# A decoder layer whose residual stream is laid out by features instead of by tokens, on one Trainium2 core

## The chip, the core and the metric

The kernel runs on one core of one Trainium2 chip. Its engines are TensorE (PE in the profile; PEld is its loading of the stationary operand), VectorE (DVE), ScalarE (ACT), GpSimd (POOL) and SyncE (SP), which here only issues DMAs. The metric is the device time of one execution in microseconds, the median of three runs.

## The reference

One layer on 1024 tokens with 1024 features, all in float32:

```
x = x + 0.5 * swiglu(rms_norm(x, ffn1_norm), w_gate, w_up, w_down)       # 2816 hidden
h = rms_norm(x, mix_norm)
q, k, v, f, sq, sk, sv, g_fox, g_sb = split(h @ w_in)
merged = sigmoid(g_fox) * (forgetting_attention(q, k, v, f) @ w_branch_fox)
       + sigmoid(g_sb) * (stick_breaking_attention(sq, sk, sv) @ w_branch_sb)
x = x + merged @ w_out
x = x + 0.5 * swiglu(rms_norm(x, ffn2_norm), ...)
x = x + sigmoid(rms_norm(x, ple_norm) @ w_ple_gate) * (p @ w_ple_proj)
rms_norm(x, g) = x * rsqrt(mean(x*x over features) + 1e-6) * g
```

There are four norms over features; each is followed by a product that sums over features. `p` has 256 columns.

## The kernel before

**Operands.** A product needs both operands with the summed dimension on the 128 partitions. To keep float32 accuracy each operand is split into a high part, rounded to the format that TensorE takes (`f32r`), and a low part, the difference; a product is high x high + high x low + low x high, three matmuls. ACT makes high parts by a copy (line 112, in line 136 for whole weight tiles), DVE or POOL the low parts by a subtraction (line 113, line 146).

**Layout.** The residual `X` is two tiles, one for each half of the tokens, with tokens on partitions: `[128 tokens, 4 token tiles, 1024 features]`. The normed activation is wanted with features on partitions. So for each tile of 128 tokens `norm_stat` squares the row on ACT (line 206, the sum comes with it), POOL adds EPS and raises to -0.5 (210, 211), `norm_mul` scales by the token's factor and the gain row on DVE (214), and `turn` transposes the eight 128x128 blocks on TensorE (219) into PSUM, from where `norm_post` (or `norm_high` and `norm_low`) splits them. The gain is loaded as a row spread over 128 partitions.

**Feed-forward.** Gate and up products and the down product use a Strassen-like scheme: seven products of blocks (numbers 1 to 7) for eight, with sums and differences of blocks of activations (`combo_a`, `_t`, `_l`, `_u`, `_s`, `_d`, `_e`) and of weights (`sums`, `last_sum`). `prep(n, m)` splits the weight operand of product `m` of weight block `n`; `product` issues its twelve matmuls (464), `plain` the first blocks without the scheme (419), which need the normed first half alone (`half` 0) and both halves' sums (`half` 1). Half 0 of the norm is called `N[0]`, half 1 `N[1]`; products on `N[1]` come later, so its norm stands between the first products.

**Down pass.** `make_down` runs seven steps for each of three chunks of hidden rows; a step has four `matmuls(t)` of twelve (359) and four `evict(t)` that add the bank to `X` (367, or 365 in the output projection, which uses the same code with one chunk). The stationary operand is the activation `act`, the moving one the weight `wt`, so the result has tokens on partitions. In the last chunk the norm of the next stage starts: statistics of half 0 at step 4, `norm_mul` at step 5, `norm_post` of half 0 and the statistics of half 1 at step 6. While the pass runs, the tail of the stage loads and splits the next weights (`load_v`, `split_v`, `ple_load`, `ple_split` and so on).

**Places of the norms.** Four stretches of the run are spoken of. A: the entry, `first_entry`, in which `p` is projected (`project`, 1208) while `x` is loaded and normed, and then `products`. B: the end of the first feed-forward, with the first units of `w_in` (`nat_steps`, 691) behind it. C: the output projection, `second_entry`, and `products`. D: the end of the second feed-forward, with the gate of the last stage behind it (`ple_steps`, 1490). In B and D the norm of half 1 is woven into the products of half 0 by `posts` and `weave`.

**Order.** From the entry of a feed-forward to the end of its tail the code runs under `manual_schedule`: each engine takes its instructions in the order in which they are written. Outside it (attention, the last eight gate units) a planner orders them, with TensorE's order pinned by `pe`. Tiles come from pools by tag; a tag has a fixed number of buffers (`BUFS`: PT 3, WL 3, H 4, Q, KH, KL, GF, RN 2), and a new tile waits for a free one.

## Time and profile before

| what | value |
|---|---|
| median of three runs | 2262.65 us (2262.49 to 2262.69) |
| profiled execution | 2262.69 us |
| its span in the trace | 2261.0 us |
| DMA | 276.01 MB, mean 122 GB/s |
| matmuls and transposes on TensorE | 11441 |

The profile comes from one execution. Its page gives the busy time of each engine, the chain of work that ended last, and groups of instructions by source line with their mean duration in ns and the idle time before them. In the view by time a row has start, duration, engine, line, operation and how many instructions were merged; in the chain in order of time a row has start, duration and what ran. Recorded matmuls overlap (389 ns each for 512 columns), so their spacing is what counts, not their duration. Busy time of PEld lies beside that of PE.

### The profile page before, as it was taken

The numbers are of one execution on the slowest core, as the hardware profiler recorded it, in microseconds if no ns is written. First come the engines' busy times: TensorE is split into PE (matmuls) and PEld (weight loads), VectorE is DVE, ScalarE is ACT, GpSimd is POOL, SyncE is SP. The second block draws the span as 40 slices with busy tenths as digits, with TensorE's granted clock in tenths as the row PEclk, the third lists the DMA queues.
The fourth block names the chain that finished last, engine by engine and source line by source line (L and its number), as shares of the span: only waits on it lengthen the run. The fifth ranks groups of instructions, "written<-read, shape, count | busy, mean of one in ns | idle before, by whom it ended". The sixth has DMA issues, their size and how long they took to land.

```text
span 2261.0 us, 30610 instructions
## 1 busy us (share of the span) xinstructions
PE 2243.2 (99%) x11441; PEld 1907.6 (84%) x11441; DVE 1468.5 (65%) x2206; ACT 975.4 (43%) x1740; POOL 820.2 (36%) x756
## 2 busy tenths in 40 slices
PE   9999999999999999999999999999999999999999
PEld 7888888888889999998988888888888888888887
DVE  7854545497873565656666676889655555778752
ACT  6433333343343555545456564246333333434431
POOL 1244444310024556645455654410544443200111
PEclk9999999999999999999999999999999999999999
DMA  7223232474432222222124236822423232756132
GB/s 261 79 94 117 90 120 84 163 282 147 164 125 56 77 85 71 75 62 75 43 71 117 62 121 206 304 104 61 140 84 126 84 126 80 261 194 216 62 101 93
DMA packets 186373, 276.01 MB, mean 122 GB/s; under 512 B 27112, under 2 KB 109288, under 8 KB 186224
## 3 DMA queue, kind: packets, MB, share of 16 engines
q1 hardware_dynamic: 186224, 274.05, 36.3%
q8 instruction: 90, 1.47, 0.3%
q14 instruction: 59, 0.48, 0.1%
HBM read 190.35 MB, written 75.27 MB: 117 GB/s over the span
## 4 chain that ended last, share of the span: by engine, by line
PE 95%; DVE 3%; ACT 1%; issue 1%; DMA 0%; POOL 0%; SPq 0%; POOLq 0%; DVEq 0%; ACTq 0%
PE ps L464 35%; PE ps L359 21%; PE ps L699 11%; PE ps L691 7%; PE ps L1490 4%; PE ps L1159 4%; PE ps L963 3%; PE ps L941 3%; PE ps L419 1%; PE ps L890 1%; PE ps L889 1%; PE ps L219 1%; PE ps L1208 1%; DVE RN L865 1%; DVE H L113 0%
## 5 line engine op out<-in xcount | busy, mean ns | idle before, releaser
L359 PE MATMUL ps<-H,H 128*128 128x512 f32 x2184 | 497.7, 389 | 1.2 <-DVE X L367 1.2
L359 PEld LDWEIGHTS ps<-H,H 128*128 128x128 f32 x2184 | 409.4, 188 | 86.7 <-issue 2.0
L464 PE MATMUL ps<-H,WL 128*128 128x512 f32 x1008 | 239.3, 389 | 0.8 <-ACT WL L112 0.8
L464 PEld LDWEIGHTS ps<-H,WL 128*128 128x128 f32 x1008 | 189.1, 188 | 40.5 <-ACT WL L112 1.2
L699 PE MATMUL ps<-H,WH 128*128 128x512 f32 x768 | 210.4, 401 | 1.0 <-DVE PT L814 1.0
L699 PEld LDWEIGHTS ps<-H,WH 128*128 128x128 f32 x768 | 136.2, 188 | 23.8 <-DVE PT L814 1.5
L146 POOL TENSOR_TENSOR WL<-Y,WH 128x512 fp32r<-128x512 f32 (+1 forms) x10 | 14.4, 1470 | 382.6 <-ACT WH L136 382.6
L944 DVE TENSOR_TENSOR PT<-ps,PT 128x512 fp32r<-128x512 f32 (+1 forms) x160 | 101.1, 633 | 73.0 <-ACT PT L943 71.8
L146 POOL TENSOR_TENSOR WL<-RAW,WH 128x512 fp32r<-128x512 f32 (+1 forms) x104 | 122.6, 1200 | 59.8 <-ACT WH L136 46.7
L464 PE MATMUL ps<-H,Q 128*128 128x512 f32 x600 | 143.1, 389 | 0.0
L367 DVE SCALAR_TENSOR_TENSOR X<-ps,X 128x512 f32<-128x512 f32 x168 | 109.1, 687 | 50.9 <-PE ps L359 50.9
L691 PE MATMUL ps<-WH,H 128*128 128x256 f32 (+1 forms) x896 | 132.9, 287 | 1.9 <-ACT RN L748 0.7
L464 PEld LDWEIGHTS ps<-H,Q 128*128 128x128 f32 x600 | 112.6, 188 | 23.4
L943 ACT CAST PT<-ps 128x512 fp32r<-128x512 f32 (+1 forms) x160 | 87.4, 549 | 93.6 <-PE ps L941 92.0
L464 PE MATMUL ps<-X,WL 128*128 128x512 f32 x504 | 121.1, 389 | 0.0
L691 PEld LDWEIGHTS ps<-WH,H 128*128 128x128 f32 x896 | 117.0, 190 | 4.0 <-PE ps L890 1.0
L464 PEld LDWEIGHTS ps<-X,WL 128*128 128x128 f32 x504 | 94.6, 188 | 19.6
L699 PE MATMUL ps<-H,WL 128*128 128x512 f32 x384 | 108.5, 399 | 0.0
L963 PE MATMUL ps<-PT,X 128*128 128x256 f32 (+1 forms) x640 | 104.1, 282 | 3.1 <-DVE PT L944 3.1
L963 PEld LDWEIGHTS ps<-PT,X 128*128 128x128 f32 x640 | 94.2, 190 | 14.6 <-DVE PT L944 5.3
L902 POOL TENSOR_TENSOR T<-T,l 128x128 f32<-128x128 f32 (+3 forms) x64 | 73.2, 1148 | 89.9 <-DVE l L901 87.5
L260 POOL TENSOR_TENSOR PT<-GF,RN 128x512 f32<-128x512 f32 x20 | 33.1, 1657 | 186.0 <-DVE GF L507 101.8
(402 smaller groups left out, 4719.7 us busy)
## 6 DMA issues: line engine op xcount, KB each, us to landing
hidden<-PT SPq DMA_DIRECT2D x40, 512.0 KB, 3.1
WH<-in_ffn_w_gate_dram SPq DMA_DIRECT2D x38, 512.0 KB, 4.8
Q<-hidden SPq DMA_DIRECT2D x24, 512.0 KB, 6.3
hidden<-RN SPq DMA_DIRECT2D x22, 512.0 KB, 2.6
RAW<-in_w_in_dram SPq DMA_DIRECT2D x22, 512.0 KB, 4.3
KH<-in_ffn_w_up_dram SPq DMA_DIRECT2D x20, 512.0 KB, 6.3
KL<-in_ffn_w_up_dram SPq DMA_DIRECT2D x20, 512.0 KB, 7.0
T<-in_ffn_w_down_dram SPq DMA_DIRECT2D x20, 512.0 KB, 4.6
```

What stands on the lines that cost most here:

```text
L146: ins = eng_lo.tensor_sub(lo[part], raw[part], f(hi[part]))
L359: pe(nc.tensor.matmul(groups[g][t][:], act[:, a, k, t * P:(t + 1) * P], wt[:, b, k, :], start=(fresh and n == 0), stop=(i in (6, 1, 4) and ...
L367: nc.vector.scalar_tensor_tensor(xs, groups[g][t][:], scale, xs, ALU.mult, ALU.add)
L464: pe(nc.tensor.matmul(ps[:], hl[:, a, k, :], rhs(m, b, k), start=(first and i == 0), stop=(final and i == 11), skip_group_check=True))
L691: pe(nc.tensor.matmul(ps[:, :n], hT[t // 4][a][:, k, (t % 4) * P:(t % 4 + 1) * P], w[k // 4][b][:, k % 4, :n], start=(i == 0), stop=(i == ...
L699: pe(nc.tensor.matmul(ps[:], w[a][:, k, :], hT[half][b][:, k, :], start=(i == 0), stop=(i == 23)))
L902: nc.gpsimd.tensor_mul(T[:, :n], T[:, :n], l[:].broadcast_to([P, n]))
L943: high = nc.scalar.copy(pt[:, 0, :width], ps[:, :width])
L944: low = nc.vector.tensor_sub(pt[:, 1, :width], ps[:, :width], f(pt[:, 0, :width]))
L963: pe(nc.tensor.matmul(o, lh, r, start=(kpair == c and i == 0), stop=(kpair == 0 and i == 3)))
L1159: pe(nc.tensor.matmul(ps[:], w[a][:, k, :], yT[g][b][:, k, half * 512:half * 512 + 512], start=(i == 0), stop=(i == 11)))
L1490: pe(nc.tensor.matmul(ps, hT[t // 4][a][:, k, (t % 4) * P:(t % 4 + 1) * P], pl["w"][d, k // 2][b][:, k % 2, cs], start=(i == 0), stop=(i = ...
```

## The change

The residual stays with features on partitions from input to output. `x`, the four gains and the result are laid out by the host, outside the measured time: `X[half]` is `[128, 8 feature tiles, 512 tokens]`.

- Down passes, output projection, the projection of `p` and the last gate exchange their operands: the weight is stationary, the activation moving, so results have features on partitions. Counts and shapes of the matmuls stay.
- The gain is a column of eight values per partition, loaded once (`gain_load`).
- A norm no longer transposes tiles. `squares` squares a pair of feature tiles on ACT and adds it to a running sum on POOL or DVE, `fold` adds the pair's two halves, and `token_scales` turns the four 128x128 blocks on TensorE, so that tokens are on partitions and DVE can sum over the 128 columns; then EPS, the power on POOL, and a copy that spreads each token's factor over 128 columns. `spread` turns that back; then `scaled` multiplies each tile by the factors in PSUM and the gain, and `high` and `low` split it.
- Norms of whole halves take the place of those of single token tiles, at other points of the written order. `combo_*` work on pairs of feature tiles (`i` = 0, 1) instead of token tiles (`q` = 0 to 3), and `combo_a` no longer has transposes; its part of line 113 moves to POOL.
- The squares of the first two pairs of half 0 move to step 1 of the last chunk, when these tiles are done.

```diff
+    def squares(N, j, tag, eng=nc.gpsimd):
+        t = slot(tag, [P, 2, 512])
+        nc.scalar.activation(t[:], N["x"][:, 2 * j:2 * j + 2, :], AF.Square, scale=D ** -0.5)
+        if "sum" in N:
+            eng.tensor_add(N["sum"][:], N["sum"][:], t[:])
...
+            N["sum"] = t
+    def fold(N, eng=nc.vector):
+        a = N["sum"]
+        eng.tensor_add(a[:, 0, :], a[:, 0, :], a[:, 1, :])
+    def turn(src, ps):
+        for t in range(4):
+            pe(nc.tensor.transpose(ps[:, t * P:(t + 1) * P], src[:, t * P:(t + 1) * P], identf[:]))
+    def token_scales(N, new_bank):
+        ps = new_bank()
+        turn(N["sum"][:, 0, :], ps)
+        ss, rs = stat([P, 4], "ss"), stat([P, 4], "rs")
+        nc.vector.reduce_sum(ss[:], ps[:].rearrange("p (t d) -> p t d", t=4), axis=AX.X)
+        nc.vector.tensor_scalar(ss[:], ss[:], EPS, None, ALU.add)
+        nc.gpsimd.tensor_tensor(rs[:], ss[:], mhalf[:, 0:4], ALU.pow)
+        nc.vector.tensor_copy(N["sum"][:, 1, :].rearrange("p (t d) -> p t d", t=4), rs[:].unsqueeze(2).broadcast_to([P, 4, P]))
+    def spread(N, new_bank):
+        N["r"] = new_bank()
+        turn(N["sum"][:, 1, :], N["r"])
+    def scaled(N, j, tag):
+        h = N["h"][j] = slot(tag, [P, 2, 512])
+        for c in range(2):
+            k = 2 * j + c
+            nc.vector.scalar_tensor_tensor(h[:, c, :], N["r"][:], N["g"][:, k:k + 1], N["x"][:, k, :], ALU.mult, ALU.mult)
+    def high(N, *js):
+        for j in js:
+            nc.scalar.copy(target(N, j, 0), N["h"][j][:])
+    def low(N, j, eng=nc.vector):
+        eng.tensor_sub(target(N, j, 1), N["h"][j][:], f(target(N, j, 0)))
...
-                        pe(nc.tensor.matmul(groups[g][t][:], act[:, a, k, t * P:(t + 1) * P], wt[:, b, k, :], ...
+                        pe(nc.tensor.matmul(groups[g][t][:], wt[:, b, k, t * P:(t + 1) * P], act[:, a, k, :], ...
...
         def last_norms(i, t):
+            if i == 1 and t % 2:
+                squares(nxt[0], t // 2, ("PT", "RN")[t // 2])
+            elif i == 4 and t % 2:
+                squares(nxt[0], 2 + t // 2, ("GF", "RN")[t // 2], (nc.gpsimd, nc.vector)[t // 2])
+                if t == 3:
+                    fold(nxt[0])
             elif i == 5:
+                if t % 2:
+                    squares(nxt[1], 2 + t // 2, ("GF", "RN")[t // 2])
+                if t == 1:
+                    token_scales(nxt[0], ps1)
+                elif t == 3:
+                    spread(nxt[0], ps1)
+                    scaled(nxt[0], 0, "PT")
+                    scaled(nxt[0], 1, "PT")
+                    high(nxt[0], 0, 1)
             elif i == 6:
+                if t == 0:
+                    scaled(nxt[0], 2, "KH")
+                    low(nxt[0], 0, nc.gpsimd)
+                elif t == 1:
+                    scaled(nxt[0], 3, "KL")
+                    squares(nxt[1], 0, "KH")
+                    high(nxt[0], 2)
+                    low(nxt[0], 1)
+                elif t == 2:
+                    high(nxt[0], 3)
+                    low(nxt[0], 2)
+                else:
+                    low(nxt[0], 3)
+                    squares(nxt[1], 1, "KL", nc.vector)
+                    fold(nxt[1])
...
+    def second_half(N, at, new_bank):
+        return {at[0]: [lambda: token_scales(N, new_bank)],
+                at[1]: [lambda: spread(N, new_bank), lambda: scaled(N, 0, "PT"), lambda: scaled(N, 1, "PT"), lambda: high(N, 0, 1)],
+                at[2]: [lambda: scaled(N, 2, "PT"), lambda: scaled(N, 3, "Q"), lambda: low(N, 0, nc.gpsimd)],
+                at[3]: [lambda: low(N, 1), lambda: high(N, 2, 3)],
+                at[4]: [lambda: low(N, 2), lambda: low(N, 3)]}
```

The entry (A), as it is written after the change, from the first units on (loads and stores left out):

```
        project([(m, 0) for m in range(4)], ps2)
        split_p("p", k, 1, nc.vector)                        # k = 0, 1
        squares(N[0], 0, "PT"); squares(N[0], 1, "WL")
        project([(0, 1)], ps1)
        split_p("w", k, 1, nc.gpsimd)                        # k = 0, 1
        squares(N[0], 2, "WL", nc.vector)
        project([(1, 1)], ps1)
        squares(N[0], 3, "WL", nc.vector); fold(N[0])
        project([(2, 1)], ps1); project([(3, 1)], ps1)
        token_scales(N[0], ps1)
        project([(4, 0)], ps2); project([(4, 1)], ps2); project([(5, 0)], ps2)
        spread(N[0], ps1); scaled(N[0], 0, "PT")
        project([(5, 1)], ps2); high(N[0], 0); scaled(N[0], 1, "PT")
        project([(6, 0)], ps2); low(N[0], 0); high(N[0], 1); scaled(N[0], 2, "PT")
        F["prep"](0, 1)
        project([(6, 1)], ps2); low(N[0], 1); high(N[0], 2); scaled(N[0], 3, "GF")
        project([(7, 0)], ps2); low(N[0], 2); high(N[0], 3)
        project([(7, 1)], ps2)
        F["prep"](0, 2); low(N[0], 3)
        squares(N[1], 0, "PT"); squares(N[1], 1, "PT")
        F["plain"](0, 0, (0,))
        squares(N[1], 2, "PT"); squares(N[1], 3, "GF", nc.vector); fold(N[1])
        F["prep"](0, 5)
        F["plain"](0, 0, (1,))
        F["prep"](0, 4); F["sums"](1, nc.vector)
        products(F)
```

and the common part of A and C:

```
    def products(F):
        F["load"](2)
        token_scales(N[1], ps2)
        F["plain"](1, 0, (0,)); F["prep"](1, 1); F["plain"](1, 0, (1,))
        spread(N[1], ps2)
        F["m"](0, 2); F["a"](0); F["prep"](1, 2)             # m: scaled of pairs
        ps = F["product"](1, 1)
        F["m"](1, 3); F["a"](1); F["prep"](1, 5)
        F["evict"](1, 1, ps); F["t"](0)
        ps = F["product"](1, 2)
        F["t"](1); F["l"](0); F["evict"](1, 2, ps); F["prep"](2, 1); F["l"](1)
        F["plain"](0, 1); F["u"](0); F["s"](0, 6); F["prep"](2, 2)
        F["plain"](1, 1); F["u"](1); F["s"](1, 6); F["prep"](1, 6)
```

In C, `second_entry` places the norm steps at the same steps of the projection as `last_norms` does, with `finished` stores of row pairs between them; behind the last step stand `load(1)`, `prep(0, 2)`, `plain(0, 0, (0,))`, `prep(0, 5)`, `plain(0, 0, (1,))`, `prep(0, 4)`, `sums(1)` and `products`.

## The prediction

> **What bounds the kernel now.** First the page's busy shares and its chain of work that ended last.

> ```profile
> span 2261.0 us, 30610 instructions
> PE 2243.2 (99%) x11441; PEld 1907.6 (84%) x11441; DVE 1468.5 (65%) x2206; ACT 975.4 (43%) x1740; POOL 820.2 (36%) x756
> PE 95%; DVE 3%; ACT 1%; issue 1%; DMA 0%; POOL 0%; SPq 0%; POOLq 0%; DVEq 0%; ACTq 0%
> ```

> TensorE is the bound: it is 95% of the chain and busy for 99% of the span. So two things count: TensorE instructions that go, and pauses that come. Next the chain in order of time, for the four places where a norm stands: A (entry, 14 to 72 us), B (end of the first feed-forward, 660 to 702), C (output projection to second feed-forward, 1510 to 1563), D (end of the second, 2151 to 2193).

> ```profile
> 13.71 6.02 PE ps L1208 x24
> 24.22 2.77 PE ps L1208 x12
> 27.86 2.74 PE ps L1208 x12
> 71.52 389.26 PE ps L464 x1716
> 460.77 125.14 PE ps L359 x552
> 594.67 70.97 PE ps L359 x312
> 1445.16 70.72 PE ps L359 x312
> 1557.24 394.40 PE ps L464 x1740
> 2085.53 70.97 PE ps L359 x312
> ```

> A matmul of 512 columns takes 125.14/552 = 0.227 us where activations are stationary (line 359) and 389.26/1716 = 0.227 where weights are (line 464). So exchanging the operands of the down passes, of the two projections and of the last gate moves nothing by itself: I cost it at 0, and the added and removed loads of weights are equal in number. Twelve matmuls take 2.72; from 24.22 to 27.86, 3.64, lie twelve and one group of eight transposes, so such a group costs 0.90 to 0.92; I take 0.90, 0.113 each.

> Old pauses of TensorE: from 13.71 to 71.52 lie 216 matmuls (49.0) and eight groups (7.2): 57.8 less 56.2 is 1.6. From 1515.88, where the row of 1445.16 ends, to 1557.24 lie 144 matmuls (32.7) and eight groups: 1.5. In B and D I see 0.5 together. Sum 3.6.

> **What is removed and added.**

> ```profile
> 0.00:2261.00 2261.00, 32.77 (x256) 29.41 (x256) 1.00 0.37 122
> ```

> That is line 219 alone in the view of stretches: 256 transposes. Each of four norms has two halves; after the change a half turns its folded sums (4) and its scales (4), 64 in all. 192 x 0.113 = **21.6 us leave the path**. The four gain broadcasts, 512 KB each, and the row-wise stores change no row of the chain (DMA 0%): 0, hidden by matmuls. The small gain load on ACT's queue lies in ACT's wait for p at the start: 0, 0.5 if that cover is gone.

> Against this stands latency. Until now a token tile was normed by itself, and a group of transposes waited for one square and one power. Now nothing of a half can be scaled before all eight feature tiles have been squared, added, folded, turned, reduced, raised to -0.5, spread out and turned back. The prices:

> ```profile
> 14.07 1.07 ACT L206 ACTIVATE PT<-X 128x1024 f32<-128x1024 f32 x1
> L206 ACT ACTIVATE PT<-X 128x1024 f32<-128x1024 f32 x10 | 10.6, 1058 | 11.3 <-DVE X L365 10.3 <-DVE X L367 1.0
> L112 ACT CAST WL<-WH 128x512 fp32r<-128x512 f32 x44 | 27.2, 617 | 0.0
> L113 DVE TENSOR_TENSOR H<-GF,H 128x1024 fp32r<-128x1024 f32 x16 | 19.5, 1222 | 0.0
> L367 DVE SCALAR_TENSOR_TENSOR X<-ps,X 128x512 f32<-128x512 f32 x168 | 109.1, 687 | 50.9 <-PE ps L359 50.9
> L261 POOL TENSOR_TENSOR PT<-PT,GF 128x512 f32<-128x512 f32 x20 | 26.5, 1325 | 1.6
> L755 POOL TENSOR_TENSOR RN<-RN,qkss 128x1024 f32<-128x1024 f32 x8 | 15.2, 1906 | 0.6
> 16.07 3.53 POOL L113 TENSOR_TENSOR H<-T,H 128x512 fp32r<-128x512 f32 x2
> L211 POOL TENSOR_TENSOR rs<-ss,mhalf 128x1 f32<-128x1 f32 x32 | 20.0, 627 | 29.8 <-ACT ss L208 27.8
> L753 POOL TENSOR_TENSOR qkss<-qkss,mhalf 128x16 f32<-128x16 f32 x8 | 23.3, 2908 | 26.6 <-DVE qkss L752 26.6
> L749 DVE TENSOR_REDUCE qkss<-PT 128x4 f32<-128x256 f32 x24 | 10.0, 416 | 11.3 <-ACT PT L747 11.1
> ```

> A square or cast of a pair of tiles is 1.06 on ACT; a pair is 1.2 on DVE, a single tile 0.6 in a run; `scaled` of a pair is two of the form of line 367, 1.2. Not shown is POOL's add of a pair: 1.9 (row of 755) to 3.5 (two tiles beside a busy DVE); I take 2.5, near two of line 261. The power of 4 columns lies between 0.6 and 2.9; along the line through 1 and 16 columns 1.1. Reduction of 512 columns and spreading copy: 0.4 to 0.7 each; I take 0.65. Reduce, add of EPS, power and copy are then 2.6 with their hand-overs. In these stages each engine's instructions stand in the trace as they are written, so what stands behind a waiting instruction waits too.

> *A, first half.* TensorE is through with four units at 13.7 + 24 x 0.227 = 19.2. The first square still starts at 14.07, the second ends at 16.1, POOL's add at 18.6, two adds and the fold on DVE (1.2, 1.2, 0.7) at 21.9; `token_scales` stands in TensorE's queue and waits **2.8**. From 22.0 three units follow, with `token_scales` until 26.5, then `spread` (27.0) and five units: `plain` starts at 33.8 and its second part is due at 36.5. DVE starts `scaled` at 27.4; four of them (4.8), two `low` (2.4) and two single tiles (1.2) bring it to 36.1 with a wait of 0.3 for ACT. On ACT the last `high`, an eviction and `prep(0,2)` follow, to 38.2: **1.8**.

> *A, second half.* Its squares stand on ACT behind that, 38.1 to 42.1; POOL's two adds end at 45.2, DVE's add and fold at 47.1. `token_scales` stands ahead of `plain(1, ...)`, though that has nothing to do with it; TensorE is free at 41.0: **6.2**.

> *A, after the spread.* From there to product (1, 6) TensorE has 96 matmuls, 21.8. DVE has four `scaled`, six differences of `t` and `l`, four of `u`, three low parts of pairs and five single tiles: 17 pairs at 1.2 and 5 singles at 0.6 make 23.4. It waits for ACT's high part of a pair three times (1.1 each), and product (1, 6) for two casts at the end (1.8): 28.5. The excess of **6.7** falls at product (1, 2) (`prep(1,2)` behind two casts, 1.6), `plain(0,1)` (1.2) and product (1, 6) (3.9). Before, this preparation was spread between all the `plain` parts. A together: 17.5.

> *B and D, first half.* In D:

> ```profile
> 2134.31 5.71 POOL L146 TENSOR_TENSOR WL<-Y,WH 128x512 fp32r<-128x512 f32 x4 [173.20 <-ACT WH L136]
> 2140.22 0.69 DVE L367 SCALAR_TENSOR_TENSOR X<-ps,X 128x512 f32<-128x512 f32 x1 [2.03 <-PE ps L359]
> 2143.06 2.36 DVE L113 TENSOR_TENSOR H<-RAW,H 128x1024 fp32r<-128x1024 f32 x2 [2.15 <-ACT H L112]
> 2145.34 2.35 DVE L113 TENSOR_TENSOR H<-Q,H 128x1024 fp32r<-128x1024 f32 x2
> 2156.11 1.03 PEld L219 LDWEIGHTS ps<-identf,PT 128*128 128x128 f32 x8
> ```

> POOL is in the low halves of weights until 2140.0; behind them stands the add of the third pair, to 2142.5. DVE waits for it, adds and folds to 2144.5, then makes the four low parts (4.6) and two evictions: 2150.3; reduce to copy: 2152.9. The last pass would start at 2156.1 - 5.4 = 2150.7, and the `spread` after four transposes more; it waits **1.7**. B has the same queue: **1.7**. The last `low` stands behind the last eviction on DVE and holds up the first unit after the pass: in B it ends at 676.2, and the unit, started at 673.8, wants it 14 matmuls of 0.12 in, at 675.5: 0.7; in D, where matmuls are longer, it is POOL's low part of the gate weights, behind two adds, that comes 0.5 late. The second halves lie beside 17 and more matmuls per step and cost 0, in B 0.7, since POOL's power stands ahead of the low halves that free the next weights' buffers. B 3.1, D 2.2.

> *C.*

> ```profile
> 1499.60 0.69 DVE L365 TENSOR_TENSOR X<-ps,X 128x512 f32<-128x512 f32 x1 [2.03 <-PE ps L359]
> 1515.49 1.02 PEld L219 LDWEIGHTS ps<-identf,WL 128*128 128x128 f32 x8
> 1534.73 1.28 ACT L427 ACT_TABLE_LOAD   x1
> WH<-in_ffn_w_gate_dram SPq DMA_DIRECT2D x38, 512.0 KB, 4.8
> ```

> No low halves of weights stand on POOL here. The fourth pair is evicted at 1500.3; square, add and fold end at 1503.4, four low parts and two evictions at 1509.3, the copy at 1511.9. `spread` is due at 1515.5 - 5.4 + 0.5 = 1510.6: **1.3**. The last fold ends at 1527.2, behind it the low part of `prep(0,2)`, which TensorE wants at 1526.9: **0.9**. The table load comes on ACT ahead of `prep(0,4)`, now at 1532.2; DVE's `sums` and the reduction stand behind that, the copy ends at 1537.4, `spread` is due at 1535.5: **1.9**. After it 6.7 as in A. C: 10.8. On SP two stores of finished rows, waiting for evictions until 1513, now stand ahead of the load of the first weights; it lands 5 to 6 us later, and its cast is due at 1521.8: 0, and each us beyond that cover of 2 would be one more.

> **Sum.** -21.6 (transposes) - 3.6 (old pauses) + 17.5 + 3.1 + 10.8 + 2.2 (new pauses, 33.6) = **+8.4**. The profiled run took 2262.69 for its span of 2261.0; 2262.69 + 8.4 = 2271.1, against the median of 2262.65.

> **Rivals.**
> *Cheap steps.* With POOL's add at 1.9, the power at 0.6 and copy and reduction at 0.4, A loses 1.8 of its pauses, B and D 1.6 each at their spread, C 2.0 at two: 2271.1 - 7.0 = 2264.1, no change within 0.2%, which is about what a measurement of this kernel can tell from none. For it: two of three prices are guessed. Against: the 6.7 twice, made of known prices.

> *The turns don't hold up the queue (faster).* If the products written behind the waiting transposes run ahead of them, the pauses of 2.8, 6.2, 1.7, 1.7, 1.3 and 1.9 go, 15.6: 2255.5. It is a gain of over 0.2% once 13 of the 15.6 go. For it:

> ```profile
> 687.34 1.05 ACT L136 CAST WH<-RAW 128x1024 fp32r<-128x1024 f32 x1 [2.17 <-DMA RAW<-in_w_in_dram]
> 688.29 0.64 ACT L112 CAST X<-ps 128x256 fp32r<-128x256 f32 x2
> ```

> this cast of the attention stage runs ahead of an eviction that is written before it. Against: in all four places TensorE's groups of line 219 stand exactly where they are written.

> *A cold TensorE (slower still).*

> ```profile
> 1.27 4.62 PE L195 MATMUL ps<-T 128*128 128x512 bf16 x11 [1.27 <-DVE T L192]
> 0.00:5.90 5.90, 4.62 (x11) 1.50 (x11) 1.04 (x3) 2.27 (x4) 1.52 (x10) 1.00 0.67 231
> PE ps L963 <- DVE PT L944: 3.1, 5, 1.6
> ```

> The eleven matmuls of 512 columns at the start take 0.42 each, half speed, for 4.6 us. If the pause of 6.2 in A brings this back, the 4.6 us behind it do half their work: +2.3, 2273.4; with the two pauses of 3.9 too, 2278. Against: of TensorE's waits the longest is 1.6 us (last number of the last row, from the view of waits), so the trace can't show it. [...]

> *Not what it says:* a stationary operand of weights could load slower in these passes; the two rates of 0.227 speak against it.

> **How the numbers follow.** Forecast 0.40; cheap steps 0.22; turns don't hold 0.13; cold 0.23; dearer steps (POOL's adds at 3.5 add 1 in A's first half, 2 in its second, 1 each in B and D; 2276) 0.02. Faster 0.13, same 0.22, slower 0.65. The range runs from 2262, below the cheap steps, to 2278, the cold end; under it lies the faster rival.

> **What would show it.** Right: 64 transposes of line 219's kind; TensorE idle for about 6 us at 41 to 47 us, released by DVE's fold; waits of 1 to 2 us at each spread in B, C, D; product (1, 6) waiting some 4 us in A and C; the first long stretch of line 464 starting at 82 us in place of 71.5. Wrong: that stretch starting before 72, or a pause of the main loops (75 to 590, 1570 to 2080), where I expect none.

## The result, and the profile after

The changed kernel takes 2298.03 us (median of 4 runs, 2297.55 to 2298.56) against 2262.67 for the kernel before: ratio 1.0156, 95% interval 1.0139 to 1.0174, 35.4 us slower where 8.4 were forecast. The direction was right, the size was four times too small. First the page of the changed kernel, its head and the shares of its chain:

```profile
span 2295.9 us, 30051 instructions
...
PE 2238.4 (97%) x11249; PEld 1894.2 (83%) x11249; DVE 1491.6 (65%) x2190; ACT 960.2 (42%) x1628; POOL 862.6 (38%) x732
...
PE 84%; DVE 7%; issue 6%; POOL 2%; ACT 1%; DMA 1%; POOLq 0%; ACTq 0%; DVEq 0%
```

TensorE has 192 instructions fewer, as forecast. But some 21 us of work went and its busy time fell by 4.8 only (from 2243.2): part of the rest runs slower. And its share of the chain fell from 95% to 84%. The chain in order of time (start, duration, what ran):

```profile
89.51 391.77 PE ps L456 x1716
481.28 125.13 PE ps L351 x552
...
1594.81 391.77 PE ps L456 x1716
```

Line 351 is the down pass: 125.13/552 = 0.227 us, as before, so the exchange of operands costs nothing. The first long stretch starts at 89.51 where it started at 71.52. Who waited, by the view of TensorE's waits (in all, times, longest):

```profile
PE ps L215 <- DVE PT L211: 9.7, 2, 5.8
PE ps L456 <- ACT WL L112: 9.7, 2, 4.9
PE ps L694 <- DVE log_f L733: 5.4, 1, 5.4
PE ps L456 <- ACT PT L112: 3.3, 2, 1.7
PE ps L215 <- DVE PT L225: 2.8, 3, 1.1
PE ps L215 <- DVE GF L211: 2.2, 1, 2.2
```

Line 215 is a turn or spread, 211 the fold, 225 the copy of the scales. There are six pauses of 2.2 to 5.8 us. The view of stretches, from the end of each of these six pauses on (length, TensorE busy, granted clock, DMA share, GB/s):

```profile
23.71:30.00 6.29, 6.29 (x25) 0.77 0.81 270
50.37:56.00 5.63, 5.63 (x20) 0.68 0.59 186
89.51:98.00 8.49, 8.49 (x26) 0.68 0.00 0
713.20:718.00 4.80, 4.80 (x29) 0.69 0.44 113
1594.81:1602.00 7.19, 7.19 (x21) 0.63 0.01 2
2206.32:2213.00 6.68, 6.68 (x26) 0.74 0.31 110
```

TensorE is busy throughout, at a clock of 0.63 to 0.77. Length times what is missing to 1.00: 1.5 + 1.8 + 2.7 + 1.5 + 2.7 + 1.7 = 11.9 us lost to slow clock. In the kernel before, the view shows 1.00 in every stretch of 2 us from 14 to 104.

The stages' ends are read from the view in order of time: A ends where the first feed-forward's down passes begin, B where the output projection begins, C where the second feed-forward's down passes begin, D with the span. The kernel before: 460.6, 984.4, 506.5 and 309.5 us. All runs of this study but e_pauses (2424.48 in one execution), each place against that (profiled execution; the ratio is to the kernel before, measured beside it). The profiled execution can lie 2 us from the median of its kernel (2286.66 in e_dve, 2264.39 in e_repair3, 2261.17 in e_repair4), so the places need not add up to the difference of the medians.

| run | time, us | ratio, 95% | A | B | C | D |
|---|---|---|---|---|---|---|
| forecast | 2271.1 | | +10.5 | -2.6 | +3.9 | -3.5 |
| changed kernel | 2298.03 | 1.0139-1.0174 | +20.5 | +4.1 | +10.4 | 0.0 |
| e_warm | 2289.71 | 1.0104-1.0134 | +15.1 | +4.1 | +8.3 | -1.6 |
| e_late_scales | 2293.08 | 1.0120-1.0150 | +22.3 | 0.0 | +9.2 | -1.1 |
| e_early | 2295.99 | 1.0133-1.0167 | +19.8 | +4.1 | +8.3 | 0.0 |
| e_swap | 2295.83 | 1.0132-1.0166 | +18.8 | +4.7 | +9.1 | 0.0 |
| e_dve | 2289.23 | 1.0100-1.0130 | +12.9 | +3.5 | +7.4 | -0.2 |
| e_free | 2290.28 | 1.0105-1.0139 | +17.6 | +3.5 | +8.4 | -2.1 |
| e_repair | 2282.76 | 1.0075-1.0105 | +15.2 | -0.6 | +4.9 | +0.3 |
| e_repair2 | 2284.07 | 1.0076-1.0110 | +12.5 | +3.1 | +8.8 | -2.7 |
| e_repair3 | 2262.55 | 0.9992-1.0011 | +4.8 | -0.3 | +0.7 | -3.5 |
| e_repair4 | 2258.98 | 0.9976-0.9994 | -0.5 | +0.8 | +1.6 | -3.4 |

The theory from these views: a pause of TensorE is paid twice, by its length and by a slow clock behind it; and the pauses are longer than forecast because DVE and POOL slow each other and because whole chains on DVE and ACT start late. The rivals: pauses cost their length only; or the waits at the turns alone are the matter.

### The profile page after: what moved, and what is told of

The parts are those of the page before. It is cut to its first block, busy times and chain, and to the rows that moved or that the text cites. A ratio compares the mean times of both kernels' runs of the same rounds, so it can differ in the third digit from the quotient of the medians.

```text
span 2295.9 us, 30051 instructions
## 1 busy us (share of the span) xinstructions
PE 2238.4 (97%) x11249; PEld 1894.2 (83%) x11249; DVE 1491.6 (65%) x2190; ACT 960.2 (42%) x1628; POOL 862.6 (38%) x732
## 4 chain that ended last, share of the span: by engine, by line
PE 84%; DVE 7%; issue 6%; POOL 2%; ACT 1%; DMA 1%; POOLq 0%; ACTq 0%; DVEq 0%
PE ps L456 34%; PE ps L351 14%; PE ps L702 11%; PE ps L694 7%; PE ps L1514 4%; PE ps L1169 3%; PE ps L966 3%; PE ps L944 3%; PE ps L893 1%; PE ps L892 1%; DVE H L113 1%; DVE RN L868 1%; POOL PT L205 1%; POOL WL L146 0%; ACT H L112 0%
## 5 line engine op out<-in xcount | busy, mean ns | idle before, releaser
L456 PE MATMUL ps<-H,WL 128*128 128x512 f32 x1008 | 244.5, 395 | 9.7 <-ACT WL L112 9.7
L456 PEld LDWEIGHTS ps<-H,WL 128*128 128x128 f32 x1008 | 192.7, 191 | 51.1 <-ACT WL L112 10.6
L146 POOL TENSOR_TENSOR WL<-RAW,WH 128x512 fp32r<-128x512 f32 (+1 forms) x104 | 122.5, 1199 | 61.7 <-ACT WH L136 48.1
L359 DVE SCALAR_TENSOR_TENSOR X<-ps,X 128x512 f32<-128x512 f32 x168 | 108.3, 687 | 45.4 <-PE ps L351 45.4
L456 PEld LDWEIGHTS ps<-H,Q 128*128 128x128 f32 x600 | 112.6, 188 | 23.4
L205 POOL TENSOR_TENSOR PT<-PT,RN 128x1024 f32<-128x1024 f32 x2 | 4.8, 2402 | 296.8 <-ACT RN L203 296.8
L702 PE MATMUL ps<-H,WL 128*128 128x512 f32 x384 | 108.5, 399 | 0.0
## 6 DMA issues: line engine op xcount, KB each, us to landing
hidden<-PT SPq DMA_DIRECT2D x40, 512.0 KB, 3.1
WH<-in_ffn_w_gate_dram SPq DMA_DIRECT2D x38, 512.0 KB, 5.4
Q<-hidden SPq DMA_DIRECT2D x24, 512.0 KB, 6.2
hidden<-RN SPq DMA_DIRECT2D x22, 512.0 KB, 2.6
RAW<-in_w_in_dram SPq DMA_DIRECT2D x22, 512.0 KB, 4.3
KH<-in_ffn_w_up_dram SPq DMA_DIRECT2D x20, 512.0 KB, 6.1
KL<-in_ffn_w_up_dram SPq DMA_DIRECT2D x20, 512.0 KB, 6.9
T<-in_ffn_w_down_dram SPq DMA_DIRECT2D x20, 512.0 KB, 4.8
```

The lines of the kernel that those rows point to most:

```text
L146: ins = eng_lo.tensor_sub(lo[part], raw[part], f(hi[part]))
L359: nc.vector.scalar_tensor_tensor(xs, groups[g][t][:], scale, xs, ALU.mult, ALU.add)
L456: pe(nc.tensor.matmul(ps[:], hl[:, a, k, :], rhs(m, b, k), start=(first and i == 0), stop=(final and i == 11), skip_group_check=True))
L702: pe(nc.tensor.matmul(ps[:], w[a][:, k, :], hT[half][b][:, k, :], start=(i == 0), stop=(i == 23)))
```

## Experiments

### What a pause costs

```diff
...
+                if m == 2 and n in PAUSE:      # n = 4, 6, ... 16
+                    for _ in range(PAUSE[n]):
+                        nc.vector.tensor_add(dl[:], dl[:], identf[:])
+                    pe(nc.tensor.transpose(bank("av")[:, 0:P], dl[:], identf[:]))
```

> The changed kernel with seven more pauses of TensorE in each of the two main loops: behind the eviction of product (n, 2), n = 4, 6, ... 16, DVE makes 1, 6, 12, 18, 24, 32, 48 dependent additions of 128x128 (about 0.15 us each), and TensorE must transpose their result; the output is not touched. Theory 'clock': a pause of less than about 3 us costs its own length, and the matmuls behind it keep their 0.227 us; behind the longer ones (18 additions and more) the granted clock reads 0.5 and some 9 to 12 matmuls are spaced 0.45 us, so each of them costs a further 2 to 2.7 us, which does not grow with the length of the pause. Rival 'length': a pause costs its length only; the slow stretches of the changed kernel come from operands that arrive late, and here, where all operands are there, the matmuls behind every pause are spaced 0.227 us.

Measured: an addition took 0.29 us, so the pauses came out at 1 to 16 us. In the view by time, three of the pauses (last bracket) and the twelve matmuls behind each:

```profile
184.20 0.30 PE L612 MATMUL ps<-identf,dl 128*128 128x128 f32 x1 [2.70 <-DVE dl L611]
184.26 3.02 PE L459 MATMUL ps<-T,Q 128*128 128x512 f32 x12
...
1752.76 0.30 PE L612 MATMUL ps<-identf,dl 128*128 128x128 f32 x1 [2.70 <-DVE dl L611]
1752.82 4.57 PE L459 MATMUL ps<-T,Q 128*128 128x512 f32 x12
...
430.68 0.45 PE L612 MATMUL ps<-identf,dl 128*128 128x128 f32 x1 [16.39 <-DVE dl L611]
430.78 5.28 PE L459 MATMUL ps<-T,WL 128*128 128x512 f32 x12
```

Twelve matmuls take 3.0 behind a pause of 1 us, and 4.5 to 5.3 behind every one of the ten pauses of 4.7 to 16.4: 1.5 to 2.3 lost, without growth with length. The pause of 2.70 is the telling one: the same pause, same place in the loop, cost nothing the first time and 1.55 the second. So it also matters when a pause falls. "Length" is out. The border of about 3 us was an estimate of mine that no run shows: 2.70 was enough.

In the trace of the changed kernel half clock is granted in six stretches of 3.41, 6.83, 6.83, 3.41, 6.83 and 3.41 us, from 23.24, 47.14, 88.10, 712.74, 1593.37 and 2207.77 on; these starts are 7, 12, 183, 258 and 180 times 3.4133 us apart. What decides is seen when the view of stretches is cut into steps of 3.41 us, one of which ends where the half clock of 1753.24 begins (length, TensorE busy, granted clock, DMA share, GB/s):

```profile
179.70:183.11 3.41, 1.80 (x8) 1.00 0.40 159
183.11:186.52 3.41, 2.32 (x11) 1.00 0.00 0
...
1749.83:1753.24 3.41, 0.71 (x5) 1.00 0.10 42
1753.24:1756.65 3.41, 3.41 (x10) 0.50 0.02 5
```

The first pause of 2.70 lies across the border of two steps, 1.6 us idle in one and 1.1 in the other, and the clock stays. The second lies within one step, and the next step is granted 0.50. In all eleven traces of this study that show half clock, its stretches begin on one such grid, whose phase differs between executions, and last one to five steps (3.4 or 6.8 us in the changed kernel, 17.1 around the pause of 16.4). At full clock, every step with 1.91 us or more of idle time was followed by half clock and none with 1.77 or less; 1.81 (in e_repair4) was, 1.89 (in e_dve) was not. In the changed kernel the border lies between 1.66 (from 60.79 on, clock 1.00 behind it) and 1.95 (from 2204.36 on, 0.50 behind it).

### The same pauses, filled

```diff
+    def warm(n):
+        z = identf[:].bitcast(BF16)
+        ps = bank("av")
+        for _ in range(n):
+            pe(nc.tensor.matmul(ps[:, 0:256], z[:, 0:P], z, start=True, stop=True))
...
+        warm(34)
         token_scales(N[0], ps1)
...
+                if s == 2:
+                    warm(41)
                 evict(n, m, product(n, m))
```

> The changed kernel with small bf16 matmuls of the identity, whose result nobody reads, in the six long pauses: 34 ahead of the first turn in A, 48 ahead of the second, 41 ahead of product (1, 6) in A and in C, 46 ahead of the 97th matmul of the attention's first units in B, 17 ahead of the second turn in D. At 0.107 us each they fill 3.6, 5.1, 4.4, 4.9 and 1.8 us of pauses of 4.0, 5.75, 4.85, 5.4 and 2.2. Theory 'clock': what TensorE waits for is ready no sooner, but the stretches behind at a granted clock of 0.5 go, which I sum up to 1.5 + 1.8 + 2.7 (A), 1.5 (B), 2.7 (C) and 1.7 (D), 11.9 us: about 2286. Rival 'length': the time stays at 2298, or rises by the up to 3 us by which the small matmuls can run past the wait.

Measured: 2289.71, 8.3 us less, and a mean granted clock of 1.000. The small matmuls took 0.11 us each (48 in 5.41, 34 in 3.88). By time, the changed kernel's matmuls behind the first pause in A and in product (1, 6):

```profile
24.44 5.40 PE L1219 MATMUL ps<-H,H 128*128 128x512 f32 x18
...
89.51 8.25 PE L456 MATMUL ps<-H,WL 128*128 128x512 f32 x24 [4.84 <-ACT WL L112]
```

and the same with the pauses filled:

```profile
23.80 4.37 PE L1228 MATMUL ps<-H,H 128*128 128x512 f32 x18
...
86.16 5.73 PE L462 MATMUL ps<-H,WL 128*128 128x512 f32 x24 [0.42 <-ACT WL L112]
```

The time of A fell by 5.4, of C by 2.1, of D by 1.6, of B not at all: there 1.6 us of waiting were left behind 5.2 of filling, since ACT's cast of the loaded weights came 229.5 us after the start of the down passes, in the changed kernel 228.2; why it came later is not shown. So the slow clock is worth 8 to 12 us of the excess (8.3 regained here, 11.9 by the granted clock). It is not all of it: 27 us over the kernel before stay.

### B and D: POOL's queue

```diff
-            side[48] = [lambda: mx["qk"].update(w=[wsplit(...)])]
+            side[12] = [lambda: mx["qk"].update(w=[wsplit(...)])]
...
-            side = second_half(N_[1], (20, 37, 46, 56, 66), ps2)
+            side = second_half(N_[1], (40, 57, 66, 76, 86), ps2)
```

> The changed kernel with the splitting of the first query and key weights in B at step 12 of the woven units instead of step 48, ahead of the second half's turn, and the second half's norm in D 20 steps later (steps 40, 57, 66, 76, 86). Theory 'queue': in B the power stood in POOL's queue ahead of the low halves that free the buffers of the next weights, and the wait of 5.4 us at the first query and key unit ended with that load; now POOL makes the low halves some 5 us sooner, the wait falls under 1 us and the slow matmuls behind it (1.5) go: about 6 us. In D the turn waited 2.2 us for DVE's fold beside POOL's low halves; 20 steps later the sum is there: 2.2 and 1.7 of slow clock go. Together 2288. Rival 'load': the load of the weights takes its time whenever it is asked for, and DVE and POOL get in each other's way at another place; the wait in B stays above 3 us, 2294 to 2298.

The chain in B, by time in the changed kernel (the bracket is the idle time before and its releaser):

```profile
701.58 1.02 POOL L224 TENSOR_TENSOR rs<-ss,mhalf 128x4 f32<-128x4 f32 x1 [7.71 <-DVE ss L223]
702.57 2.71 POOL L146 TENSOR_TENSOR GF<-RAW,T 128x512 fp32r<-128x512 f32 x2
...
709.32 1.04 ACT L136 CAST WH<-RAW 128x1024 fp32r<-128x1024 f32 x1 [7.38 <-DMA RAW<-in_w_in_dram]
...
712.16 0.64 ACT L112 CAST X<-ps 128x256 fp32r<-128x256 f32 x2
```

POOL stands idle for 7.7 us ahead of the power, with the low halves behind it. They free RAW, its load lands at 709.3, and ACT, waiting for that load, has the evictions behind it that TensorE needs. With the split ahead of the turn, this wait reads 1.8 in place of 5.4 and B takes 4.1 less (6 were expected): "queue" holds. D took 1.1 less, of the 3.9 expected: the turn no longer waits, but two waits of 1.2 for POOL's low halves took its place. A was not edited and came out 1.8 us longer; the reason is in its rows. Behind the same wait for the fold (4.01 here, 3.99 in the changed kernel) the same 18 matmuls took 6.43 here and 5.40 there, the clock at 0.50 for 6.8 us in place of 3.4. Differences of a microsecond or two in A are within this play of the clock.

### A and C: what product (1, 6) hangs on

```diff
         F["load"](2)
-        token_scales(N[1], ps2)
         F["plain"](1, 0, (0,))
+        token_scales(N[1], ps2)      # A; in C ahead of the second part of plain(0, 0),
+                                     # and the spread ahead of plain(1, 0)
...
```

> The changed kernel with the second half's turns at other places in TensorE's order: in A, the first part of plain(1, 0) ahead of the turn and only the second between turn and spread; in C, the turn ahead of the second part of plain(0, 0) and the spread ahead of plain(1, 0), with the first two scaled pairs. Nothing else changes. Theory 'chain': from the spread on, DVE and ACT need 31.5 us to product (1, 6), in A as in C, and TensorE has less to do there, so product (1, 6) starts as much sooner as the spread does: in A about 4 us sooner, in C 3 to 5. The end comes 7 to 9 us sooner, 2289 to 2291, and another 1 to 3 if a pause gets short enough to keep the clock. Rival 'late casts': product (1, 6) waits for something that does not hang on the spread (weights, buffers that come free); then both starts stay within 1 us of where they are, and the time at 2295 to 2298.

Spread and product (1, 6) in A, by time, in this run:

```profile
50.59 3.43 PE L411 MATMUL ps<-H,WL 128*128 128x512 f32 x8 [3.89 <-DVE WL L113]
...
57.07 0.60 PE L215 MATMUL ps<-identf,PT 128*128 128x128 f32 x4
...
88.52 3.78 PE L456 MATMUL ps<-H,WL 128*128 128x512 f32 x8 [4.88 <-ACT WL L112]
```

And the spread in the changed kernel:

```profile
58.04 0.60 PE L215 MATMUL ps<-identf,PT 128*128 128x128 f32 x4
```

The product stood at 89.51 there. So the spread moved by 0.97, not by 4, and the product by 0.99: from spread to product 31.45 and 31.47 us. By itself this does not decide, for both moves and the time, 2295.99, lie within the rival's bounds too. The other runs that leave the work behind the spread alone decide it for A: with the spread anywhere from 54.71 (e_warm) to 59.50 (e_late_scales), the product stands 31.45 to 31.46 behind it. In C "chain" failed as it was put: the spread came 6.2 sooner (1557.12 for 1563.30), the product 1.7, so 36.0 us lie between them in place of 31.5. DVE was still at the sums of weights written ahead of `scaled`, which began 2.6 sooner only, and ACT's casts stood behind a SiLU that waited for TensorE. So the chain starts when DVE and ACT are free, not with the spread. In A the spread came so little sooner by an oversight of mine: the first part of plain(1, 0) wants a low half that stands behind the fold on DVE, so it waited 3.9 in the turn's stead.

```diff
-        seqn = [(1, 5), (2, 1), (1, 6), (2, 2), (1, 7), ...
+        seqn = [(1, 5), (2, 1), (2, 2), (1, 6), (1, 7), ...
```

> The changed kernel with one exchange in the order of products, in both feed-forwards: (2, 2), whose operands are ready, ahead of (1, 6). Theory 'chain': product (1, 6) starts as before 31.5 us behind the spread, when DVE and ACT are through, but TensorE does the twelve matmuls of (2, 2), 2.7 us, inside the pause: it shrinks from 4.85 us to 2.1 in A and in C, together 5.4 us: 2292.6. If a pause of 2.1 lets the clock stand, the 2.7 us of slow matmuls behind each go as well: 2287. Rival 'moved wait': the low half of (2, 2)'s weights or its accumulator is as late as (1, 6)'s operand, the wait of 4.85 stands ahead of (2, 2) and the time stays within 1 us of 2298.

```profile
89.06 3.01 PE L456 MATMUL ps<-H,WL 128*128 128x512 f32 x12 [2.14 <-ACT WL L112]
94.11 4.61 PE L456 MATMUL ps<-X,WL 128*128 128x512 f32 x12 [2.04 <-ACT Y L476]
```

The pause shrank from 4.84 to 2.14 as forecast, and a new one of 2.04 stands one product later: (1, 7) adds to the bank of (1, 6) and waits for its eviction on ACT (line 476), which (2, 2) had covered. 2.2 us of 5.4 or more were left, and the clock still fell (12 matmuls in 4.61). "Moved wait" was right, at a place that I had not named.

### DVE and POOL side by side

```diff
-            split(pair("12", 0, i), pair("12", 1, i), wa(i)[:], nc.scalar, nc.gpsimd)
+            split(pair("12", 0, i), pair("12", 1, i), wa(i)[:], nc.scalar, nc.vector)
...
-                squares(nxt[0], 2 + t // 2, ..., (nc.gpsimd, nc.vector)[t // 2])
+                squares(nxt[0], 2 + t // 2, ..., nc.vector)      # the same in C, and in A for every addition
...
```

> The changed kernel with work of the norms moved from POOL to DVE: in A all additions of squares, in B, C and D the third addition of the first half (each 1.2 us on DVE against 2.4 on POOL), and the low halves of the pair '12' (two of 1.2 against 2.4). Theory 'shared': DVE's additions and low halves on operands in SBUF took 2.2 us in place of 1.2 wherever POOL worked beside them, so POOL's help was paid for by DVE; with POOL out of the way they read 1.2, the second turn in A comes some 2.5 us sooner and the first some 1.5, the spreads in B, C and D lose their waits of 1.1, 0.7 and 1.0, and product (1, 6) is at most 0.5 us later behind the spread: 2290 to 2293. Rival 'relief': POOL works beside DVE at no cost, the 2.2 us have another reason and stay; then each chain behind the spread grows by 2.4 us, which eats the gain of the turns: 2296 to 2299.

By time, a low half of `T` on DVE in the changed kernel, with POOL's low half beside it:

```profile
67.77 2.40 POOL L113 TENSOR_TENSOR X<-Q,X 128x1024 fp32r<-128x1024 f32 x1 [4.16 <-ACT X L112]
...
69.06 2.20 DVE L113 TENSOR_TENSOR T<-KL,T 128x1024 fp32r<-128x1024 f32 x1 [1.12 <-ACT T L112]
```

and both on DVE:

```profile
62.09 1.22 DVE L113 TENSOR_TENSOR X<-Q,X 128x1024 fp32r<-128x1024 f32 x1
63.30 1.22 DVE L113 TENSOR_TENSOR T<-KL,T 128x1024 fp32r<-128x1024 f32 x1
```

DVE's 2.20 until 71.26 end 1.1 after POOL's 2.40 until 70.17, which is nearly a whole 1.22, as if it had begun its work when POOL was through. POOL's help brought nothing. With DVE alone the way from spread to product (1, 6) is 29.6 us (53.24 to 82.83) in place of 31.5, though DVE has two more low halves in it; the second turn comes 4.7 sooner. The run gained 8.8 us where I expected 5 to 8: "shared". Part of it is the clock: the time lost to half clock fell from 11.9 to 8.2 us in the profiled executions. Not every instruction of DVE grew longer beside POOL: `scaled`, which reads PSUM, kept 0.68 an instruction in B (4 in 2.73 from 704.89) beside two low halves on POOL (705.24 to 707.77), and all 64 of the changed kernel (line 235) are recorded at 0.73 to 0.75.

### All turns free of waiting

```diff
-        turn(N["sum"][:, 0, :], ps)
+        turn(N["x"][:, N.get("early", 0), :], ps)
...
-        nc.vector.tensor_scalar(ss[:], ss[:], EPS, None, ALU.add)
+        nc.vector.tensor_scalar(ss[:], ss[:], 1e6, None, ALU.add)
...
-        turn(N["sum"][:, 1, :], N["r"])
+        turn(N["x"][:, N.get("early", 0), :], N["r"])
```

> The changed kernel whose two turns of each half read a finished tile of the residual in place of the folded sums and the spread scales, with a large constant for EPS: the statistics of the norms are left out of the result, every instruction stays, but TensorE no longer waits for a square, an addition, a power or the copy. Theory 'two parts': the pauses at turns and spreads go (4.0 and 5.75 in A, 1.1 in B, 0.7 and 0.4 in C, 1.0 and 2.2 in D: 15.2) with the slow clock behind three of them (1.5 + 1.8 + 1.7), about 20 us: 2278; the 15 us that are then left over the kernel before come from the work behind the spreads (product (1, 6), casts and low halves) and from B's weights. Rival 'all latency': once the scales are there sooner, what stands behind them is in time too, and the pauses at product (1, 6) shrink as well: 2266 to 2272. Rival 'queue': DVE and ACT hold the adds and folds in the same order, so TensorE only comes to wait some matmuls later for the same engines: 2288 to 2296.

Measured: 2290.28, and TensorE's waits in A (to 90 us) now are:

```profile
PE ps L456 <- ACT WL L112: 4.9, 1, 4.9
PE ps L411 <- DVE WL L113: 3.9, 1, 3.9
PE ps L411 <- ACT WL L112: 3.5, 2, 2.7
```

The turns wait for nothing, and `plain` (line 411) waits for casts and low halves that stand behind the squares and folds on ACT and DVE: 7.7 of 20 us gained, "queue". So taking the turns out of its way does not win back the latency of the norm; what is left to change is the order on ACT and DVE.

### Putting the order right

Four kernels with the changed kernel's arithmetic in another order, with some additions, low halves and evictions on another engine, each built on the last. The first, in its core (`b` is the cast and low half of '12', taken out of `a`):

```diff
+        F["plain"](0, 0, (0,))
+        token_scales(N[1], ps2)
+        F["plain"](0, 0, (1,))
+        F["plain"](1, 0, (0,))
+        spread(N[1], ps2)
+        F["m"](0)
+        F["plain"](1, 0, (1,))
+        F["prep"](1, 2); F["b"](0); F["m"](1); F["b"](1); F["m"](2, 3)
...
+        seqn = [(2, 1), (1, 5), (2, 2), (1, 6), (1, 7), ...
+        squares(N[1], 1, "Q", nc.vector)       # A: ahead of project([(4, 1)], ps2)
```

> The changed kernel with its steps put in another order, the arithmetic as it was. A: the low half of the second weights ahead of the squares, the squares of half 1 made while ACT stands idle at 20 to 27 us, their turn between the two parts of plain(0, 0), additions mostly on DVE. A and C: spread between the parts of plain(1, 0), the four scaled pairs in one run, the casts and low halves behind them, products (2, 1), (1, 5), (2, 2) ahead of (1, 6). B, D: as in the run with later scales, and the third addition on DVE. Theory (chains that start late, and the clock behind the pauses): product (1, 6) comes 14 to 17 us sooner in A and 9 to 12 in C, the two stretches of slow clock behind it (2.7 each) go, B gives 4 to 6 and D 3 to 4: 2253 to 2265. Rival: what is put elsewhere meets POOL, ACT or buffers that are not free there, a wait of several us comes up at another place, and the time stays above 2270.

2282.76: B as expected, C half of it, D nothing, A 5 in place of 14 and more. In A the copy of the scales took 2.56 us beside POOL's additions, and `plain` waited 4.6 for a low half.

```diff
+        token_scales(N[1], ps2, [lambda: F["prep"](0, 4), lambda: F["prep"](1, 1)])   # between power and copy
+        F["prep"](1, 2)                        # ahead of plain(1, 0, (1,))
+        seqn = [(2, 1), (1, 5), (2, 2), (1, 6), (2, 6), (1, 7), ...
+        wsplit(raws["qk"][kh], 4, 256, tags[kh], nc.vector)
```

> The run e_repair with the waits mended that its trace shows. A: POOL's additions of half 1 no longer beside the copy that spreads the scales (it took 2.56 us beside them, 0.43 alone) but beside the scaled pairs, which read PSUM and kept their 0.7 us there; two low parts of weights between power and copy; evictions of the last units on ACT. A and C: the cast of prep(1, 2) ahead of the SiLU that waited for TensorE, product (2, 6) between (1, 6) and (1, 7). B, D: low halves one step earlier, additions of half 1 on DVE, in B the low halves of the query and key weights on DVE. Theory (late chains, POOL beside DVE, and the clock behind pauses are all that the change lost): A loses pauses of 4.5, 4.6, 1.6 and 2.2 and the slow clock behind the first two, 14 to 18 us; B 2, C 3 to 5, D 1 to 2: 2257 to 2263. Rival: the norm of a half needs more work of DVE than these stages have beside TensorE, wherever it is put; then the pauses come up again behind it and the time stays above 2272.

2284.07, the rival's figure, for three reasons. POOL's additions still met the copy:

```profile
24.87 7.42 POOL L205 TENSOR_TENSOR RN<-RN,Q 128x1024 f32<-128x1024 f32 x3
...
24.93 2.61 DVE L227 COPY PT<-rs 128x512 f32<-128x512 f32 x1 [1.13 <-POOL rs L224]
```

The pause at product (1, 6) fell to 1.7, but DVE had no gap left to catch up, and 17 us later an eviction that stood behind the differences for '4' came late:

```profile
94.87 5.49 PE L458 MATMUL ps<-T,WL 128*128 128x512 f32 x12 [4.75 <-DVE Y L481]
```

And in B the low halves and additions that I had moved to DVE cost 3.7 us.

```diff
+        F["sums"](1, nc.vector)                # ahead of spread(N[1], ps2)
+        for i in range(2):
+            F["m"](i)
+            F["b"](i)
+        F["plain"](1, 0, (1,))
...
-                if s in (2, 4):
+                if s in (4, 5):                # combo_d; combo_e at 5 and 6
...
+        squares(N[1], 1, "Q")                  # A: behind project([(5, 1)], ps2)
```

> The run e_repair2 with DVE's backlog behind product (1, 6) taken apart: differences for '4' two products later, sums of the second weights ahead of the spread, POOL's additions of half 1 in A behind the copy of the scales, casts of '12' ahead of the SiLU that waits for TensorE; B and D as in e_repair, in D with the additions of half 1 behind POOL's low halves. Theory (waits at the places shown by the traces, nothing else): A loses the pause of 4.75 with its 2.7 of slow clock and some 3 of the smaller ones, C the same 4.75 with 2.7 and 1 of the others, B and D are as in e_repair or 1 to 2 better: 2258 to 2268. Rival 'DVE-bound': from the second spread to the last difference DVE has 47 us of work beside 42 of TensorE, so what is put off at one place is missing at the next: 2274 to 2282.

2262.55, in the middle of the forecast: the copy is at 0.43, no pause in A or C is over 2.6, and "DVE-bound" does not hold at this size.

```diff
+        token_scales(N[0], ps1, [lambda: squares(N[1], 1, "Q", nc.vector)])
...
+        F["prep"](0, 1); F["prep"](0, 2)       # ahead of spread(N[0], ps1)
...
+        low(N[0], 0); low(N[0], 1)             # ahead of scaled(N[0], 2, ...)
...
+            side[3] = [...]                    # B: was side[12]
```

> The run e_repair3 with the norm of half 0 in A in another order: the first two weights' parts ahead of the spread, low halves of the first two pairs ahead of the last two scaled pairs, one addition of half 1 on DVE between power and copy, the other two on POOL beside the scaled pairs only; in B the query and key weights split at step 3 of the woven units. Theory: plain(0, 0), which waited 2.6 and 0.4 us for low halves and 0.3 for weights and then ran 1.3 us of its time at half clock, comes without a pause over 1 us: A gives 4 to 5, B up to 1.8: 2256 to 2259, faster than the kernel before by 0.15 to 0.3%. Rival: from the first spread to product (1, 6) DVE is busy without a gap, so what A gains at plain(0, 0) is lost at product (1, 6), and the time stays at 2261 to 2263.

2258.98 against 2262.73, ratio 0.9985 (0.9976 to 0.9994), within the forecast: A gave 5.3. B, which should have given up to 1.8, and C took 1 more each. In B that is half clock behind the step with 1.81 us of idle time, from 685.98 on; in C the output projection waits 1.6 for its first bank in place of 0.6, in code that this edit left alone. The half clock shows in the whole time as well: where the mean granted clock was 1.000 this kernel took 2258.55 to 2259.17, where it was 0.999 2259.96 to 2261.17. The page's head:

```profile
span 2259.5 us, 30049 instructions
...
PE 2227.5 (99%) x11249; PEld 1887.9 (84%) x11249; DVE 1498.4 (66%) x2190; ACT 960.1 (42%) x1630; POOL 859.4 (38%) x730
```

TensorE has the same 11249 instructions as in the changed kernel, which took 39 us longer; it is 99% busy again, and DVE's load has hardly changed (1498.4 us for 1491.6). So the whole loss lay in the order, the choice between DVE, POOL and ACT, and the pauses, not in the amount of work that the change makes.

## Why the forecast was wrong

*Right.* 192 transposes went, the exchange of operands cost nothing, no row of the chain names a gain load or a store, the main loops have no pause of their own; the waits stand where they were forecast (first turn, second turn, plain, spreads, (1, 2), (1, 6)), and the faster rival, turns that do not hold up the queue, is out. That the new pauses at place C sum to 10.8, as forecast, is luck: the spreads took 1.1 for 3.2, the way behind the second spread 7.8 for 6.7, plain 1.8 for 0.9.

*Wrong, in order of size, for an excess of 26.5 us of the profiled span (34.9 against 8.4).*

1. **The clock, 11.9.** "If the pause of 6.2 in A brings this back ... 2273.4; with the two pauses of 3.9 too, 2278", at a chance of 0.23. The mechanism was named and priced well for one pause (2.3; measured 1.5 to 2.7). What failed was the weighing, "of TensorE's waits the longest is 1.6 us ..., so the trace can't show it": my own forecast had 33.6 us of new pauses, three of them of 3.9 and more, so it left what the trace had shown, and the slow start, at a granted clock of 1.00, was the only row that bore on it. It should have been part of the forecast. And six pauses cooled TensorE, not three: those of 4.0 and 2.2 as well, and one that I had not seen.
2. **Sizes of pauses, 7.5.** TensorE's waits at the four places sum to 41.1 against 33.6: A 19.3 for 17.5, B 7.7 for 3.1, C 10.8 for 10.8, D 3.4 for 2.2. The largest: the wait of 5.4 in B, which I had as "0.7, since POOL's power stands ahead of the low halves that free the next weights' buffers". The mechanism is that; but I did not follow it through the load and ACT's queue, which had no slack before (a wait of 1.0 stood there). Next, the first turn, 4.0 for 2.8, and the way behind the spread, 7.8 for 6.7: I had DVE's additions and low halves at 1.2, where beside POOL they took 2.1 to 2.3. I had quoted the row of two tiles that took 3.53 on POOL beside a busy DVE, and asked only what it does to POOL.
3. **4.7 that I can't assign singly.** TensorE's busy time fell by 4.8, which with the 11.9 of slow clock taken off is 16.7, for the 21.6 that I had forecast. An estimate: twelve matmuls take 3.0 behind a pause in place of 2.88, and the recorded 0.389 of the last matmul ahead of it runs 0.16 past the spacing of 0.227. That makes 0.28 for each pause besides its idle time, and 5.9 for the 21 waits more that the changed kernel has (42 for 21), enough for the 4.7; no run measured it by itself.
4. **Waits at other places, 1.7.** Two waits in the changed kernel's view have no counterpart before, one at the product of an attention branch (at 1409.60, in code that the change leaves alone), one at the start of the output projection (at 1513.91); what brings them is not shown:

```profile
PE ps L1169 <- DVE Y L986: 1.1, 1, 1.1
PE ps L351 <- DVE X L357: 0.7, 1, 0.7
```

5. **Old pauses, 0.7.** I took 3.6 off for pauses of the kernel before. At the four places its view of waits has 2.9, and these did go, or became part of the new waits:

```profile
PE ps L219 <- DVE H L113: 1.1, 2, 0.8
PE ps L691 <- DVE log_f L730: 1.0, 1, 1.0
PE ps L464 <- ACT WL L112: 0.8, 1, 0.8
```

What stays open: the last kernel's median is 3.7 us under the kernel before, of the 25 that the removed transposes and old pauses were forecast to give. Its profiled execution is 1.5 us shorter than that of the kernel before; D gives 3.4 there, and A, B and C together lose 1.9. Whether fewer operations of DVE behind the spread (in place of another order) would bring the rest was not tried. The four repairs move many steps at once, so what each move is worth is not shown.

## What to carry to other kernels

When a change takes work from the bounding engine and adds steps of one half's size on the others, price the longest dependent chain and where it starts in each in-order queue, not the engines' sums; in the trace, find the distance from the chain's first step to the product that waits, and see whether it stays the same when the start moves. Add to each pause of TensorE of about 2 us or more another 1.5 to 2.7 for the slow clock that can follow it (measured here behind pauses of 2.2 to 16.4), and fill it or keep it shorter. Splitting it is not safe: two waits of 1.2 us each in D, one close behind the other, brought half clock in e_repair and none in e_late_scales, as the steps fell. Give POOL work on SBUF only where DVE reads PSUM (`scaled` kept 0.68 beside it, a low half within SBUF took 2.20 in place of 1.22) or nothing waits for DVE.
